# Hybrid mixer and product-key expert layer: first two input columns part by part, later columns between the recurrent gates, four query columns ahead of the second norm

## The chip, the cores and the metric

The kernel runs on one core of a Trainium2 chip. The metric is device time in microseconds (us), as the median of several runs. Engines are written as the profile writes them: PE is the matmul engine TensorE (PEld its weight loads), DVE is VectorE, ACT is ScalarE, POOL is GpSimd, SP is SyncE, which here only issues DMAs. Each engine takes its instructions in the order of its own queue. An instruction whose input isn't ready holds up everything behind it on its engine.

## The reference, cut to what matters

```python
# x: 512 tokens of 1024 values; rnn width 1280 in 10 blocks of 128
n = rms_norm(h, norm_mix)
a_x, a_b, a_c, r_x, r_y, g_a, g_b = split(n @ w_in)       # 60 columns of 128
y_a = (a_b * conv3(a_c * a_x)) @ w_out_a
r_c = conv4(r_x) + rnn_conv_b
r = sigmoid(blockdiag(r_c, w_rg) + b_rg); i = sigmoid(blockdiag(r_c, w_ig) + b_ig)
a = exp(-8 * r * softplus(-lam)); b = sqrt(1 - a*a) * i * r_c
r_h = scan(h_t = a_t * h_{t-1} + b_t)
y_b = (gelu(r_y) * r_h) @ w_out_b
h = h + (sigmoid(g_a) * y_a + sigmoid(g_b) * y_b) @ w_o
n = rms_norm(h, norm_ffn)
q = n @ w_q                                               # 16 columns, 2 per head
# per head: scores against two sets of 128 keys, top 16 of each, top 16 of the sums,
# softmax, then gelu(u . n) * v over the chosen experts of 16384
out = rms_norm(h + peer(n), norm_final)
```

## The kernel before, in words

Values are kept with channels on the 128 partitions and the 512 tokens along the row, so a vector of 1024 channels is eight parts. A matmul of two float32 matrices is made of three matmuls of a narrower float type: each operand is split into a high part (a copy by ACT, `whi` for weights) and the rest (a subtraction, `wlo`, by DVE, or by POOL for `w_q`), by `split` in lines 70 to 75. `mm3` in lines 83 to 89 runs the three products for each of the eight parts. What the text calls a column is one output block of 128 channels: 24 matmuls into one of the eight PSUM banks, which `bank` hands out in rotation over a string of bank numbers. Its weights come by `weights`: a DMA of 512 KB into one of four `raw` buffers, then the split into one of three pairs of `whi` and `wlo`. So the split of a column's weights waits until the column three places earlier is done on PE.

The mixer (lines 143 to 328) starts with the six early columns 24 to 29 of `w_in` (the first six blocks of `r_x`). They are taken of x times the norm's weights (tiles `xg`, `q_hi`, `q_lo`, made part by part) ahead of the division by the root mean square. `rms` squares the eight parts on ACT, sums them on DVE and POOL, adds over the partitions by two matmuls with `ones` and ends in `rstd`. `norm` then makes the normed values `n_hi` and `n_lo`, which every later column (`proj`) reads. For each of the ten recurrent blocks j (lines 199 to 228) the column is scaled by `rstd` into `pad` (on DVE for the six early ones, a copy on ACT for the others). Then come the convolution `rc` (one step on POOL, three on DVE), its split `rch`, `rcl`, the split of the gate weights (two tiles `tmp`), the six gate matmuls of line 219, sigmoids `lr` and `lx`, a tanh `lt`, and a product `lx` on DVE. Then follow the gated convolution (columns 16, 0 and 8 plus i), the recurrence, and the output columns. At the end of the mixer stands the second norm, with `NQ` columns of queries taken ahead of it in the same manner as the early ones (lines 320 to 328). The keys are loaded into a pool that takes over the mixer's memory (lines 398 to 400).

The scheduler of the framework sets the order of each engine's queue from the order of the code and from the buffers. After the mixer come eight heads of top-16 selection (with expert columns `ut` of 384 tokens laid between), the building of the gate matrix, and 128 rounds of expert output; nothing of the code there changes but where the first queries come from.

Of the kernel before, what the change touches and what calls it, by code (L numbers as in the profile page):

```python
# [11 lines left out]
F32 = mybir.dt.float32  # L12
F32R = mybir.dt.float32r
# [28 lines left out]
GSC = 32768.0  # L42
RN = 2.0
NEARLY = 6
NQ = 2
AR = 20
AD = 4
UP = 24
# [6 lines left out]
def layer(ctx: ExitStack, tc: tile.TileContext, a):  # L55
# [39 lines left out]
    def col(name, i):  # L95
        c = C_VEC[name] + i
        return vec[:, c : c + 1]
# [13 lines left out]
    ascr = dram.tile([P, P, ND], F32, name="ascr")  # L111

    ALLB = "01234567"

    def rms(src, pool, late):
        sums = [pool.tile([P, S], F32, tag=("rch", "rcl")[i], name="ssum", bufs=1) for i in range(2)]
        for k in range(KD):
            sq, e = sums[k // 4], V if late or k < 4 else G
            if k % 4 == 0:
                A.activation(sq, src[:, k, :], AF.Square)  # L120
            else:
                s = pool.tile([P, S], F32, tag="tmp", name="sqk", bufs=3)
                A.activation(s, src[:, k, :], AF.Square)
                e.tensor_add(sq, sq, s)
        ps = bank(ALLB)
        for i in range(2):
            T.matmul(ps, ones, sums[i], start=i == 0, stop=i == 1)
        rstd = pool.tile([P, S], F32, tag="rstd", name="rstd", bufs=1)
# [13 lines left out]

    with tc.tile_pool(name="mix", bufs=1) as mp:
        h = mp.tile([P, KD, S], F32, name="h")
        w0 = weights(a["w_in"][24], KD)
        for k in range(KD):
            SP.dma_start(h[:, k, :], a["x"][:, k, :])
        p_hi = mp.tile([P, KD, S], F32R, tag="p_hi", name="n_hi")
        p_lo = mp.tile([P, KD, S], F32R, tag="p_lo", name="n_lo")

        for k in range(KD):
            n = mp.tile([P, S], F32, tag="tmp", name="xg", bufs=3)
            V.tensor_scalar_mul(n, h[:, k, :], col("nm", k))
            A.activation(q_hi[:, k, :], n, AF.Copy)  # L154
            V.tensor_sub(q_lo[:, k, :], n, q_hi[:, k, :].bitcast(F32))
        xg = ([q_hi[:, k, :] for k in range(KD)], [q_lo[:, k, :] for k in range(KD)])
        rstd = rms(h, mp, False)
        early = []
        for j in range(NEARLY):
            ps = bank(ALLB)  # L160
            mm3(ps, w0 if j == 0 else weights(a["w_in"][24 + j], KD), xg)
            early.append(ps)
        norm(h, rstd, "nm", p_hi, p_lo, mp)
        n1 = ([p_hi[:, k, :] for k in range(KD)], [p_lo[:, k, :] for k in range(KD)])

        def proj(i):
            ps = bank(ALLB)
            mm3(ps, weights(a["w_in"][i], KD), n1)
            return ps

# [73 lines left out]


        for i in range(KD):
            ps_c = proj(16 + i)
            ac = mp.tile([P, S], F32, tag="tmp", name="ac", bufs=3)
            A.activation(ac, ps_c, AF.Copy)
            ps_x = proj(i)  # L250
# [7 lines left out]
            ps_b = proj(8 + i)  # L258
# [58 lines left out]
            A.activation(hgs[0][i], n, AF.Copy)  # L317
            V.tensor_sub(hgs[1][i], n, hgs[0][i].bitcast(F32))

        rstd = rms(h, mp, True)  # L320
        qearly = []
        for i in range(NQ):
            ps = bank(ALLB)
            mm3(ps, weights(a["w_q"][i], KD, G), hgs)
            q = qp.tile([P, S], F32, tag="q", name="q", bufs=NQ)
            V.tensor_mul(q, ps, rstd)
            qearly.append(q)
        norm(h, rstd, "nf", q_hi, q_lo, mp)
# [69 lines left out]
    with tc.tile_pool(name="top", bufs=1) as rp:  # L398
# [77 lines left out]
        for hd in range(H):  # L476
            qs = []
            for s in range(2):
                if 2 * hd + s < NQ:
                    qs.append(qearly[2 * hd + s])  # L480
                    continue
                pq = bank("23")
                mm3(pq, weights(a["w_q"][2 * hd + s], KD, G), n2)
                q = rp.tile([P, S], F32, tag="q", name="q", bufs=4)
                A.activation(q, pq, AF.Copy)
                qs.append(q)
            for t in order:
                psc = bank("45")
# [219 lines left out]
```

## Time and profile before

| | |
|---|---|
| time, median of 3 runs (lowest to highest) | 1835.59 us (1829.76 to 1838.79) |
| the profiled execution: its time, its span | 1833.47 us, 1831.7 us |
| granted TensorE clock, mean of the span | 0.975 |
| busy share: PE, PEld, DVE, ACT, POOL | 95%, 83%, 70%, 41%, 18% |
| chain that ended last, by engine | PE 78%, DVE 9%, DMA 8%, ACT 3%, issue 2% |

The span runs from the first to the last instruction; 1.8 us of the profiled time lie outside it. A busy share is a mean over stages, so where an engine stands still has to be looked up by stage. The granted clock is 1.0 where TensorE has its full 2.4 GHz and 0.5 where it has 1.2 GHz.

### The profile page before, as it was taken

The page shows a single profiled execution, that of the slowest core. Times are in us where ns is not written, and L with a number is a line of the kernel's source. Part 1 is how long each engine was busy: PE and PEld are TensorE (multiplying, and loading weights), DVE is VectorE, ACT ScalarE, POOL GpSimd, SP SyncE. Part 2 cuts the span into 40 slices and gives each one's busy share as a digit, 9 for nine tenths or more (in the row PEclk, how much of TensorE's full clock was granted, in tenths as well). Part 3 has the DMA queues.
Part 4 walks back from the last instruction along what each step waited for, and adds up shares of the span by engine and source line. Part 5 has one row for each costly group of instructions (what it writes and reads, how often), then busy time and mean ns, then how long its engine had stood idle before and what let it go on. Part 6 is the DMA issues. An engine that isn't in the chain of part 4 may idle for free.

```text
span 1831.7 us, 24059 instructions
## 1 busy us (share of the span) xinstructions
PE 1748.9 (95%) x8861; PEld 1520.1 (83%) x8861; DVE 1283.4 (70%) x2340; ACT 757.9 (41%) x1282; POOL 338.3 (18%) x266
## 2 busy tenths in 40 slices
PE   7899999999989999899999799999899999899898
PEld 5588888888878888899999688888787888788786
DVE  8857543223567668999999677787676876787673
ACT  5545333222334335555555343343343433444353
POOL 1200000000035553022322112122121221122100
PEclk9899999999999999999999899999999999999899
DMA  4222322333333334679899998898898988898872
GB/s 165 80 84 92 104 86 87 103 109 98 121 104 112 104 110 150 202 275 360 345 370 368 358 324 304 310 345 308 286 319 296 328 301 289 298 346 313 288 231 77
DMA packets 147846, 410.06 MB, mean 224 GB/s; under 512 B 11536, under 2 KB 78864, under 8 KB 129680
## 3 DMA queue, kind: packets, MB, share of 16 engines
q1 hardware_dynamic: 129296, 274.30, 45.1%
q0 software_dynamic: 18432, 134.23, 19.0%
q8 instruction: 69, 1.13, 0.2%
q14 instruction: 49, 0.40, 0.1%
HBM read 366.93 MB, written 41.55 MB: 223 GB/s over the span
## 4 chain that ended last, share of the span: by engine, by line
PE 78%; DVE 9%; DMA 8%; ACT 3%; issue 2%; POOL 0%; DVEq 0%; SPq 0%; ACTq 0%; POOLq 0%
PE ps L88 53%; PE acc L618 21%; DMA back<-ascr 4%; DVE wlo L74 3%; DMA gt<-gscr 2%; PE ps L556 1%; PE ps L557 1%; ACT whi L73 1%; PE ps L490 1%; DMA gscr<-stg 1%; DVE rc L210 1%; ACT w_hi L73 1%; DVE gel L611 1%; DVE junk L386 1%; PE ps L219 1%
## 5 line engine op out<-in xcount | busy, mean ns | idle before, releaser
L73 ACT ACTIVATE whi<-raw 128x1024 fp32r<-128x1024 f32 (+1 forms) x364 | 380.9, 1046 | 714.0 <-PE ps L88 471.6
L74 DVE TENSOR_TENSOR wlo<-raw,whi 128x1024 fp32r<-128x1024 f32 (+1 forms) x328 | 392.6, 1200 | 230.7 <-ACT whi L73 229.9
L88 PE MATMUL ps<-q_hi,whi 128*128 128x384 f32 (+1 forms) x1248 | 442.9, 355 | 13.5 <-ACT q_hi L154 7.6
L88 PE MATMUL ps<-q_hi,wlo 128*128 128x384 f32 (+1 forms) x1248 | 436.9, 351 | 4.9 <-DVE wlo L74 4.9
L88 PE MATMUL ps<-q_lo,whi 128*128 128x384 f32 (+1 forms) x1248 | 436.9, 351 | 2.8 <-DVE q_lo L138 2.5
L379 POOL DMA_INDIRECT row<-uv,uidx x128 | 209.6, 1637 | 770.1 <-DVE yg L373 760.7
L618 PE MATMUL acc<-whi,w_hi 128*128 128x512 f32 x768 | 246.3, 402 | 36.2 <-ACT w_hi L73 36.2
L88 PEld LDWEIGHTS ps<-q_hi,whi 128*128 128x128 f32 x1248 | 238.1, 191 | 27.4 <-ACT q_hi L154 8.1
L88 PEld LDWEIGHTS ps<-q_hi,wlo 128*128 128x128 f32 x1248 | 238.3, 191 | 16.0 <-DVE wlo L74 5.8
L88 PEld LDWEIGHTS ps<-q_lo,whi 128*128 128x128 f32 x1248 | 238.4, 191 | 14.8 <-DVE q_lo L138 2.9
L618 PE MATMUL acc<-wlo,w_hi 128*128 128x512 f32 x768 | 243.0, 398 | 2.2 <-DVE wlo L74 2.2
L618 PE MATMUL acc<-whi,w_lo 128*128 128x512 f32 x768 | 241.7, 396 | 0.0
L618 PEld LDWEIGHTS acc<-whi,w_hi 128*128 128x128 f32 x768 | 145.7, 193 | 68.0 <-ACT w_hi L73 42.5
L618 PEld LDWEIGHTS acc<-wlo,w_hi 128*128 128x128 f32 x768 | 148.1, 193 | 34.8 <-DVE wlo L74 2.7
L618 PEld LDWEIGHTS acc<-whi,w_lo 128*128 128x128 f32 x768 | 147.5, 192 | 31.9
L88 PE MATMUL ps<-n_hi,whi 128*128 128x512 f32 x432 | 169.0, 391 | 0.0
L88 PE MATMUL ps<-n_hi,wlo 128*128 128x512 f32 x432 | 168.7, 390 | 0.0
L88 PE MATMUL ps<-n_lo,whi 128*128 128x512 f32 x432 | 168.6, 390 | 0.0
L373 DVE SCALAR_TENSOR_TENSOR yg<-row,dots,yg 128x1024 f32<-128x1024 f32 x128 | 163.6, 1278 | 0.0
L386 DVE SCALAR_TENSOR_TENSOR junk<-row,n2tok 128x1024 bf16<-128x1024 f32 x128 | 155.8, 1217 | 0.0
L74 POOL TENSOR_TENSOR wlo<-raw,whi 128x1024 fp32r<-128x1024 f32 x36 | 87.1, 2419 | 347.8 <-ACT whi L73 341.4
L88 PEld LDWEIGHTS ps<-n_hi,whi 128*128 128x128 f32 x432 | 81.5, 189 | 17.6 <-ACT lr L221 0.6
(208 smaller groups left out, 1878.2 us busy)
## 6 DMA issues: line engine op xcount, KB each, us to landing
raw<-ut SPq DMA_DIRECT2D x128, 512.0 KB, 5.5
raw<-uv SPq DMA_DIRECT2D x128, 512.0 KB, 5.8
raw<-w_in SPq DMA_DIRECT2D x60, 512.0 KB, 3.3
gscr<-stg SPq DMA_DIRECT2D x12, 2048.0 KB, 10.4
gt<-gscr SPq DMA_DIRECT2D x32, 768.0 KB, 8.1
ascr<-gel SPq DMA_DIRECT2D x62, 192.0 KB, 5.5
back<-ascr SPq DMA_DIRECT2D x62, 192.0 KB, 6.4
raw<-w_q SPq DMA_DIRECT2D x16, 512.0 KB, 3.7
```

The lines of the kernel that those rows point to most:

```text
L73: A.activation(hi, raw, AF.Copy)
L74: (lo_eng or V).tensor_sub(lo, raw, hi.bitcast(F32))
L88: T.matmul(ps, w[x][:, i, :], r[y][i], start=first and n == 0, stop=last and n == 3 * k - 1)
L210: V.scalar_tensor_tensor(rc, pad[:, w : w + S], col("rw", 4 * j + w), rc, op0=ALU.mult, op1=ALU.add)
L219: T.matmul(pg, x[:, s * P : (s + 1) * P], y, start=n == 0, stop=n == 2)
L373: V.scalar_tensor_tensor(yg, r[:, D:], dots[:, i : i + 1], yg, op0=ALU.mult, op1=ALU.add)
L379: ins = G.indirect_dma_start(out=r, out_offset=None, in_=a["uv"], in_offset=bass.IndirectOffsetOnAxis(ap=uidx[:, i : i + 1], axis=0))
L386: V.scalar_tensor_tensor(junk, r[:, :D], 1.0, n2tok, op0=ALU.mult, op1=ALU.mult, accum_out=dots[:, i : i + 1])
L490: T.matmul(psc[:, s * P : (s + 1) * P], qs[s][:, t * P : (t + 1) * P], keys[:, 2 * hd + s, :], start=True, stop=True)
L556: T.matmul(o, e2[:, ti // 2, :, ti % 2], eh[:, ti // 2, :, ti % 2], start=True, stop=False)
L557: T.matmul(o, e2[:, ti // 2, :, ti % 2], el[:, ti // 2, :, ti % 2], start=False, stop=True)
L618: T.matmul(acc[t][f], w[x][:, t * P : (t + 1) * P], vf[y][:, f * S : (f + 1) * S], start=nout == 0 and (x, y) == (0, 0), stop=nout == P - ...
```

## The change

- The first part of x is fetched ahead of the first weights, and the second column's weights after three parts. The first two columns run part by part together: as soon as a part of `xg` is split, PE takes its three products for column 24 and for column 25. Columns 26 to 29 follow whole.
- `rms` is cut into `squares` (all sums on DVE) and `inverse_rms`. The first norm's square sums come behind the third column's weights, and its two `ones` matmuls behind the third column. The six early columns keep banks 0 to 5.
- In each recurrent step j one later column is put ahead of the gates: 30 to 33, then 16, 0, 8, 17, 1, 9, in banks 0 to 5. The gates use banks 6 and 7. A column of step j needs the bank that the column six places earlier has left.
- The first step of the convolution goes from POOL to ACT.
- Four query columns (was two) run ahead of the second norm, the `ones` matmuls behind the first of them. The products with `rstd` of the third and fourth are made later, at head 1.

```diff
-NQ = 2
+NQ = 4
+NS = 2
...
-    def rms(src, pool, late):
+    def squares(src, pool):
...
-            sq, e = sums[k // 4], V if late or k < 4 else G
+            sq = sums[k // 4]
...
-                e.tensor_add(sq, sq, s)
-        ps = bank(ALLB)
+                V.tensor_add(sq, sq, s)
+        return sums
+
+    def inverse_rms(sums, names):
+        ps = bank(names)
...
+        SP.dma_start(h[:, 0, :], a["x"][:, 0, :])
         w0 = weights(a["w_in"][24], KD)
-        for k in range(KD):
+        for k in range(1, KD):
             SP.dma_start(h[:, k, :], a["x"][:, k, :])
...
+            if k == 2:
+                w1 = weights(a["w_in"][25], KD)
+        early = [bank(COLS) for _ in range(NEARLY)]
         for k in range(KD):
...
+            for ps, w in zip(early, (w0, w1)):
+                mm3(ps, [x[:, k : k + 1, :] for x in w], ([q_hi[:, k, :]], [q_lo[:, k, :]]), k == 0, k == KD - 1)
...
-        rstd = rms(h, mp, False)
-        early = []
-        for j in range(NEARLY):
-            ps = bank(ALLB)
-            mm3(ps, w0 if j == 0 else weights(a["w_in"][24 + j], KD), xg)
-            early.append(ps)
...
+        for j in range(2, NEARLY):
+            w = weights(a["w_in"][24 + j], KD)
+            if j == 2:
+                sums = squares(h, mp)
+            mm3(early[j], w, xg)
+            if j == 2:
+                rstd = inverse_rms(sums, "67")
...
+        columns = iter([o_rx + j for j in range(NEARLY, KR)] + [c + i for i in range(2) for c in (16, 0, 8)])
+        held = {}
         for j in range(KR):
-            ps = early[j] if j < NEARLY else proj(o_rx + j)
+            ps = early[j] if j < NEARLY else held.pop(o_rx + j)
...
-            G.tensor_scalar(rc, pad[:, 3 : S + 3], col("rw", 4 * j + 3), col("rb", j), op0=ALU.mult, op1=ALU.add)
+            A.activation(rc, pad[:, 3 : S + 3], AF.Identity, scale=col("rw", 4 * j + 3), bias=col("rb", j))
...
+            c = next(columns)
+            held[c] = proj(c, COLS)
             gates = []
...
-                pg = bank(ALLB)
+                pg = bank("67")
...
-            ps_c = proj(16 + i)
+            ps_c = held.pop(16 + i) if i < 2 else proj(16 + i)
...
-        rstd = rms(h, mp, True)
+        sums = squares(h, mp)
+        qps = []
+        for i in range(NQ):
+            ps = bank("0123"[i])
+            mm3(ps, weights(a["w_q"][i], KD, G), hgs)
+            qps.append(ps)
+            if i == 0:
+                rstd = inverse_rms(sums, "67")
         qearly = []
-        for i in range(NQ):
-            ps = bank(ALLB)
-            mm3(ps, weights(a["w_q"][i], KD, G), hgs)
...
+        for ps in qps[:NS]:
...
+                if n < NQ:
+                    V.tensor_mul(q, qps[n], rstd)
+                else:
```

What moves in the queues is shown at three places. The first is the start of PE's queue. Before, column 24 (`ps_163`) runs alone; its first two parts:

```order
L88 MATMUL ps_163<-q_hi_75,whi_89 128x512
L88 MATMUL ps_163<-q_lo_76,whi_89 128x512
L88 MATMUL ps_163<-q_hi_75,wlo_90 128x512
L88 MATMUL ps_163<-q_hi_75,whi_89 128x512
L88 MATMUL ps_163<-q_lo_76,whi_89 128x512
L88 MATMUL ps_163<-q_hi_75,wlo_90 128x512
```

Of the change, from the second part of column 24 (`ps_107`) on, with column 25 (`ps_108`):

```order
L89 MATMUL ps_107<-q_hi_75,whi_90 128x512
L89 MATMUL ps_107<-q_lo_76,whi_90 128x512
L89 MATMUL ps_107<-q_hi_75,wlo_91 128x512
L89 MATMUL ps_108<-q_hi_75,whi_98 128x512
L89 MATMUL ps_108<-q_lo_76,whi_98 128x512
L89 MATMUL ps_107<-q_hi_75,whi_90 128x512
L89 MATMUL ps_108<-q_hi_75,wlo_99 128x512
L89 MATMUL ps_108<-q_hi_75,whi_98 128x512
L89 MATMUL ps_108<-q_lo_76,whi_98 128x512
L89 MATMUL ps_108<-q_hi_75,wlo_99 128x512
L89 MATMUL ps_107<-q_lo_76,whi_90 128x512
L89 MATMUL ps_107<-q_hi_75,wlo_91 128x512
```

Two columns now share the parts as they come; before, the second began when the first had seven parts behind it.

The second place is PE's queue behind the last early column. Before, the gate matmuls (L219) of block 0 (`ps_430`, `ps_436`) and of block 1 (`ps_463`) stand one behind the other:

```order
L88 MATMUL ps_312<-q_hi_75,wlo_316 128x512
L219 MATMUL ps_430<-rch_420,tmp_426 128x512
L219 MATMUL ps_436<-rch_420,tmp_426 128x512
L219 MATMUL ps_430<-rcl_421,tmp_426 128x512
L219 MATMUL ps_430<-rch_420,tmp_427 128x512
L219 MATMUL ps_436<-rcl_421,tmp_426 128x512
L219 MATMUL ps_436<-rch_420,tmp_427 128x512
L219 MATMUL ps_463<-rch_453,tmp_459 128x512
L219 MATMUL ps_463<-rcl_454,tmp_459 128x512
L219 MATMUL ps_463<-rch_453,tmp_460 128x512
L219 MATMUL ps_469<-rch_453,tmp_459 128x512
```

Of the change, from the last matmul of column 30 (`ps_430`) over the gates of block 0 (L236) to column 31 (`ps_494`):

```order
L89 MATMUL ps_430<-n_hi_193,wlo_434 128x512
L236 MATMUL ps_461<-rch_420,tmp_426 128x512
L236 MATMUL ps_461<-rcl_421,tmp_426 128x512
L236 MATMUL ps_461<-rch_420,tmp_427 128x512
L236 MATMUL ps_467<-rch_420,tmp_426 128x512
L236 MATMUL ps_467<-rcl_421,tmp_426 128x512
L236 MATMUL ps_467<-rch_420,tmp_427 128x512
L89 MATMUL ps_494<-n_hi_193,whi_497 128x512
L89 MATMUL ps_494<-n_lo_194,whi_497 128x512
L89 MATMUL ps_494<-n_hi_193,wlo_498 128x512
```

Each group of six gate matmuls now has a column of 24 on either side. DVE's queue of the change for one such step (convolution of block 7, a column's weight split, product and maximum of block 5, splits of block 7):

```order
L224 SCALAR_TENSOR_TENSOR rc_863<-pad_860,vec_66,rc_863 128x512 x3
L75 TENSOR_TENSOR wlo_1010<-raw_1007,whi_1009 128x1024
L242 TENSOR_TENSOR lx_855<-lx_855,rc_799 128x512
L252 TENSOR_SCALAR lt_857<-lt_857 128x512
L75 TENSOR_TENSOR rcl_869<-rc_863,rch_868 128x512
L75 TENSOR_TENSOR tmp_875<-graw_872,tmp_874 128x256
L224 SCALAR_TENSOR_TENSOR rc_927<-pad_924,vec_66,rc_927 128x512 x3
```

The third place is PE's queue at the second norm. Before, the second query column (`ps_3689`, of `lr` and `lx`) is followed by columns that read the normed `q_hi`, `q_lo`:

```order
L88 MATMUL ps_3689<-lr_3624,wlo_3693 128x512
L88 MATMUL ps_3896<-q_hi_75,whi_3892 128x384
L88 MATMUL ps_3929<-q_hi_75,whi_3925 128x384
L88 MATMUL ps_3956<-q_hi_75,whi_3959 128x512
L88 MATMUL ps_3896<-q_lo_76,whi_3892 128x384
```

Of the change, the ends of the four query columns (`ps_3650`, `ps_3687`, `ps_3718`, `ps_3749`) with the `ones` matmuls (L132):

```order
L89 MATMUL ps_3650<-lr_3624,wlo_3654 128x512
L132 MATMUL ps_3681<-ssum_3628,ones_68 128x512
L132 MATMUL ps_3681<-ssum_3629,ones_68 128x512
L89 MATMUL ps_3687<-lr_3351,whi_3690 128x512
...
L89 MATMUL ps_3687<-lr_3624,wlo_3691 128x512
L89 MATMUL ps_3718<-lr_3351,whi_3721 128x512
...
L89 MATMUL ps_3718<-lr_3624,wlo_3722 128x512
L89 MATMUL ps_3749<-lr_3351,whi_3752 128x512
...
L89 MATMUL ps_3749<-lr_3624,wlo_3753 128x512
L89 MATMUL ps_3958<-q_hi_75,whi_3954 128x384
```

72 matmuls that don't need the norm now stand between the `ones` matmuls and the first that does; before it was 24 and a few. From row 2297 of PE's queue on (the expert columns between heads 0 and 1) its order is the same before and after, and so it is on the other engines after the first heads.

## Rows read from the trace of the kernel before

**Rows 1.** Page, part 1: busy us of TensorE (share of the span), instructions.

```profile
PE 1748.9 (95%) x8861; PEld 1520.1 (83%) x8861; DVE 1283.4 (70%) x2340; ACT 757.9 (41%) x1282; POOL 338.3 (18%) x266
```

**Rows 2.** Stretches: busy us of PE, PEld, DVE, ACT, POOL; PEclk; DMA share; GB/s.

```profile
7.58:20.91 13.33, 13.04 (x41) 9.31 (x41) 13.33 (x23) 10.05 (x18) 1.95 (x1) 1.00 0.85 311
20.91:28.28 7.37, 4.88 (x11) 2.60 (x11) 6.79 (x20) 2.48 (x3) 3.41 (x2) 0.77 0.23 81
50.72:66.42 15.70, 8.34 (x19) 4.37 (x17) 14.74 (x22) 8.61 (x13) 2.38 (x5) 0.65 0.36 117
66.42:107.19 40.77, 39.68 (x162) 30.19 (x162) 32.38 (x52) 25.01 (x43) 8.10 (x13) 0.97 0.22 71
107.19:135.30 28.11, 28.11 (x125) 23.27 (x124) 12.91 (x16) 9.98 (x14) 0.20 (x2) 1.00 0.30 94
```

**Rows 3.** Waits of PE, 50.7 to 107.2 us: total, times, longest.

```profile
PE ps L219 <- ACT rch L73: 3.6, 3, 2.9
```

**Rows 4.** Timeline of PE, 27 to 51 us: start, duration, instruction.

```profile
27.08 0.63 PE L88 MATMUL ps<-q_lo,whi 128*128 128x512 f32 x1
27.50 0.63 PE L88 MATMUL ps<-q_hi,wlo 128*128 128x512 f32 x1
...
28.51 0.40 PE L88 MATMUL ps<-q_hi,wlo 128*128 128x512 f32 x1
28.74 0.39 PE L88 MATMUL ps<-q_hi,whi 128*128 128x512 f32 x1
...
50.72 0.63 PE L219 MATMUL ps<-rch,tmp 128*128 128x512 f32 x2
```

**Rows 5.** Groups by line on DVE, 26 to 108 us: busy, mean ns, idle before.

```profile
L210 DVE SCALAR_TENSOR_TENSOR rc<-pad,vec,rc 128x512 f32<-128x512 f32 x30 | 22.4, 745 | 3.9 <-POOL rc L208 1.9 <-POOL pad L202 1.9
L74 DVE TENSOR_TENSOR wlo<-raw,whi 128x1024 fp32r<-128x1024 f32 x9 | 10.9, 1212 | 2.1 <-ACT whi L73 2.1
L74 DVE TENSOR_TENSOR rcl<-rc,rch 128x512 fp32r<-128x512 f32 x10 | 7.2, 724 | 0.4 <-ACT rch L73 0.4
L225 DVE TENSOR_TENSOR lx<-lx,rc 128x512 f32<-128x512 f32 x9 | 6.2, 686 | 4.1 <-ACT lx L221 4.1
L136 DVE SCALAR_TENSOR_TENSOR nk<-h,vec,rstd 128x512 f32<-128x512 f32 x8 | 5.5, 744 | 0.0
L138 DVE TENSOR_TENSOR n_lo<-nk,n_hi 128x512 fp32r<-128x512 f32 x8 | 5.2, 680 | 0.0
L74 DVE TENSOR_TENSOR tmp<-graw,tmp 128x256 fp32r<-128x256 f32 x10 | 4.5, 455 | 0.4 <-ACT tmp L73 0.4
L204 DVE TENSOR_TENSOR pad<-ps,rstd 128x512 f32<-128x512 f32 x6 | 4.1, 683 | 0.0
L234 DVE TENSOR_SCALAR lt<-lt 128x512 f32<-128x512 f32 x9 | 3.8, 418 | 0.0
L130 DVE RECIPROCAL rstd<-rstd 128x512 f32<-128x512 f32 x1 | 3.3, 3349 | 0.0
```

**Rows 6.** The same view on ACT, 30 to 108 us.

```profile
L221 ACT ACTIVATE lr<-ps,vec 128x512 f32<-128x512 f32 x10 | 6.9, 689 | 15.8 <-PE ps L219 15.8
L206 ACT ACTIVATE pad<-ps 128x512 f32<-128x512 f32 x4 | 2.3, 583 | 0.0
```

**Rows 7.** Timeline of PE around the second norm.

```profile
525.69 1.13 PE L127 MATMUL ps<-ssum,ones 128*128 128x512 f32 x2
...
563.93 1.16 PE L490 MATMUL ps<-keys,q 128*128 128x128 f32 x8
564.84 0.42 PE L88 MATMUL ps<-q_hi,wlo 128*128 128x384 f32 x1
```

**Rows 8.** Timeline of DVE: end of the second norm.

```profile
544.52 1.36 DVE L138 TENSOR_TENSOR q_lo<-nk,q_hi 128x512 fp32r<-128x512 f32 x2
```

**Rows 9.** Tile keys: its DMA (ns, first and last start us) and its landing.

```profile
L400 SPq DMA_DIRECT2D keys<-keys x1: 328/328/328, 546.0 to 546.0; - x1
DMA to landing us min/median/max: 4.8/4.8/4.8
```

More of the change, by code (lines that the diff above doesn't have):

```diff
@@ L113, in layer @@
     ALLB = "01234567"
-    def rms(src, pool, late):
+    COLS = "012345"
+    def squares(src, pool):
         sums = [pool.tile([P, S], F32, tag=("rch", "rcl")[i], name="ssum", bufs=1) for i in range(2)]
         for k in range(KD):
-            sq, e = sums[k // 4], V if late or k < 4 else G
+            sq = sums[k // 4]
             if k % 4 == 0:
@@ L123, in rms @@
                 A.activation(s, src[:, k, :], AF.Square)
-                e.tensor_add(sq, sq, s)
-        ps = bank(ALLB)
+                V.tensor_add(sq, sq, s)
+        return sums
+    def inverse_rms(sums, names):
+        ps = bank(names)
         for i in range(2):
             T.matmul(ps, ones, sums[i], start=i == 0, stop=i == 1)
-        rstd = pool.tile([P, S], F32, tag="rstd", name="rstd", bufs=1)
+        rstd = qp.tile([P, S], F32, tag="rstd", name="rstd", bufs=1)
         A.activation(rstd, ps, AF.Sqrt, bias=epst, scale=1.0 / D)
@@ L144, in layer @@
         h = mp.tile([P, KD, S], F32, name="h")
+        SP.dma_start(h[:, 0, :], a["x"][:, 0, :])
         w0 = weights(a["w_in"][24], KD)
-        for k in range(KD):
+        for k in range(1, KD):
             SP.dma_start(h[:, k, :], a["x"][:, k, :])
-        p_hi = mp.tile([P, KD, S], F32R, tag="p_hi", name="n_hi")
-        p_lo = mp.tile([P, KD, S], F32R, tag="p_lo", name="n_lo")
+            if k == 2:
+                w1 = weights(a["w_in"][25], KD)
+        early = [bank(COLS) for _ in range(NEARLY)]
         for k in range(KD):
@@ L155, in layer, with proj @@
             V.tensor_sub(q_lo[:, k, :], n, q_hi[:, k, :].bitcast(F32))
+            for ps, w in zip(early, (w0, w1)):
+                mm3(ps, [x[:, k : k + 1, :] for x in w], ([q_hi[:, k, :]], [q_lo[:, k, :]]), k == 0, k == KD - 1)
         xg = ([q_hi[:, k, :] for k in range(KD)], [q_lo[:, k, :] for k in range(KD)])
-        rstd = rms(h, mp, False)
-        early = []
-        for j in range(NEARLY):
-            ps = bank(ALLB)
-            mm3(ps, w0 if j == 0 else weights(a["w_in"][24 + j], KD), xg)
-            early.append(ps)
+        p_hi = mp.tile([P, KD, S], F32R, tag="p_hi", name="n_hi")
+        p_lo = mp.tile([P, KD, S], F32R, tag="p_lo", name="n_lo")
+        for j in range(2, NEARLY):
[5 more added lines that the diff above has]
+                rstd = inverse_rms(sums, "67")
         norm(h, rstd, "nm", p_hi, p_lo, mp)
         n1 = ([p_hi[:, k, :] for k in range(KD)], [p_lo[:, k, :] for k in range(KD)])
-        def proj(i):
-            ps = bank(ALLB)
+        def proj(i, names=ALLB):
+            ps = bank(names)
             mm3(ps, weights(a["w_in"][i], KD), n1)
@@ L246, in layer @@
         for i in range(KD):
-            ps_c = proj(16 + i)
+            ps_c = held.pop(16 + i) if i < 2 else proj(16 + i)
             ac = mp.tile([P, S], F32, tag="tmp", name="ac", bufs=3)
             A.activation(ac, ps_c, AF.Copy)
-            ps_x = proj(i)
+            ps_x = held.pop(i) if i < 2 else proj(i)
             pad = mp.tile([P, S + 4], F32, tag="pad", name="pad", bufs=2)
@@ L257, in layer @@
                 V.scalar_tensor_tensor(cv, pad[:, w : w + S], col("ca", 3 * i + w), cv, op0=ALU.mult, op1=ALU.add)
-            ps_b = proj(8 + i)
+            ps_b = held.pop(8 + i) if i < 2 else proj(8 + i)
             V.tensor_mul(cv, cv, ps_b)
@@ L318, in layer @@
             V.tensor_sub(hgs[1][i], n, hgs[0][i].bitcast(F32))
-        rstd = rms(h, mp, True)
+        sums = squares(h, mp)
[6 more added lines that the diff above has]
+                rstd = inverse_rms(sums, "67")
         qearly = []
-        for i in range(NQ):
-            ps = bank(ALLB)
-            mm3(ps, weights(a["w_q"][i], KD, G), hgs)
-            q = qp.tile([P, S], F32, tag="q", name="q", bufs=NQ)
+        for ps in qps[:NS]:
+            q = qp.tile([P, S], F32, tag="q", name="q", bufs=NS)
             V.tensor_mul(q, ps, rstd)
@@ L478, in layer @@
             for s in range(2):
-                if 2 * hd + s < NQ:
-                    qs.append(qearly[2 * hd + s])
+                n = 2 * hd + s
+                if n < NS:
+                    qs.append(qearly[n])
                     continue
-                pq = bank("23")
-                mm3(pq, weights(a["w_q"][2 * hd + s], KD, G), n2)
                 q = rp.tile([P, S], F32, tag="q", name="q", bufs=4)
-                A.activation(q, pq, AF.Copy)
+                if n < NQ:
+                    V.tensor_mul(q, qps[n], rstd)
+                else:
+                    pq = bank("23")
+                    mm3(pq, weights(a["w_q"][n], KD, G), n2)
+                    A.activation(q, pq, AF.Copy)
                 qs.append(q)
```

## The prediction

> **What bounds the kernel now.** I read the page first: TensorE is busy 95% of the span [rows 1], so time can be won only where PE stands, or where it runs at the lower of its two clocks. The view of stretches finds those places. From 107.19 us on the mixer is packed: 28.11 us busy of 28.11 [rows 2]. Ahead of that it is not. From 20.91 to 28.28 PE is busy 4.88 of 7.37 us at a granted clock of 0.77, from 50.72 to 66.42 it is busy 8.34 of 15.70 us at 0.65, while DVE is busy 14.74 of the 15.70 [rows 2]. The view of waits says what ends them in the second stretch, ACT's split `rch` for instance, three times and 2.9 us at the longest [rows 3]: the gates of the first recurrent blocks have no columns between them. The timeline gives PE's price at both clocks. Two matmuls of 512 tokens start 0.42 us apart at 27 us and 0.23 us apart at 28.5 us [rows 4]; the first is the 1.2 GHz level, the second the 2.4 GHz level. Around the second norm the reader sees the same in small: a `ones` product at 525.69, and the first matmul behind the scores of head 0 and the first half of head 1 only at 564.84 [rows 7].
>
> PE's queue holds the same matmuls before and after, so I compare the times at which PE reaches the same count. There are two such marks, and behind each of them PE has the same queue in both kernels.
>
> **The first mark: all 60 gate matmuls and ten later columns done.** Before, the last gate is done at 107.19, where the stretch begins [rows 2]. By the queue PE then has 118 of the 240 matmuls of the ten later columns behind it. The other 122 at 0.23 us are 28.1 us, so the mark is reached at 135.3.
>
> After, step by step:
> - The first two columns. Before, PE ran 41 matmuls in the 13.33 us from its first one on [rows 2]. I take the same pace for the 48 of the two columns: 13.33 x 48/41 = 15.6, so 23.2 us. The two columns are fed by the same splits as before and one weight split more on DVE (1.21 us, [rows 5]); the fetches differ by one place in the queue. Taken at nothing: the earlier fetch of x's first part, since the weights' split still has to end first.
> - The third column, 24 x 0.23 = 5.5, to 28.7. Behind it stand the two `ones` matmuls, 1.0 us each (the one at 525.69 lasts 1.13, [rows 7]), to 30.7. The three square sums that leave POOL for DVE cost 0.68 each like `n_lo` [rows 5]; they hide behind the third column. In the stretch from 20.91, where PE stood, POOL was still adding such sums (busy 3.41 us, [rows 2]); that stand is gone.
> - Three more columns, 72 x 0.23 = 16.6, to 47.3. Beside them runs the norm: square root 0.69 (as the sigmoid `lr` with its column operand, [rows 6]), reciprocal 3.35, eight parts at 0.744 + 0.680, and the split 1.21 of the first later column [rows 5]: 30.7 + 0.7 + 3.35 + 11.4 + 1.2 = 47.3. Both chains end together, so each us that either is longer is a us lost. The norm is what comes late next. Before, PE reached this place at 50.72 [rows 4].
> - Ten steps of a column and a pair of gates, 30 x 0.23 = 6.9 us of PE each, to 116.3. For this DVE has to keep up. A step costs it three convolution steps, a weight split, `rcl`, `lx`, `tmp`, `pad` (six times only) and `lt`: 2.24 + 1.21 + 0.72 + 0.69 + 0.46 + 0.68 + 0.42 = 6.4 us [rows 5]. That is under 6.9, though not by much. ACT was busy 25.01 of 40.77 us while the gates of eight blocks ran [rows 2]. Its new step has no row; below it lies a copy of 0.58, above it a sigmoid with a column operand, 0.69 [rows 6]. I take the upper one, since it has column operands too: ten of them are 7 us, and ahead of `lr` alone ACT was idle for 15.8 us [rows 6].
> - The tenth column's successor needs a bank that the gated convolution must first read out. It stands behind DVE's last steps; I put 1 us there. The mark comes at 117.3.
>
> The gain is 135.3 - 117.3 = 18.0 us. At best PE never waits and is at full clock throughout, 7.6 + 444 x 0.23 + 2 = 111.7, a gain of 23.6. At worst the clock and the gate chain (rivals below) take 7 and 15 us of it back.
>
> Here the Trainium skill weighs against one part. Its page "ScalarE: Activation LUTs", section "Rules for kernel authors", puts multiplies and adds on VectorE and not on ScalarE. The rows say otherwise in this place: one more convolution step of 0.745 us would lift DVE's step from 6.4 to 7.2 us, above PE's 6.9, and cost some 3 us over ten steps. I go by the rows.
>
> **The second mark: PE's row 2297, between heads 0 and 1.** Before it is reached at 564.84 [rows 7]. After, everything up to the second `ones` product at 525.69 is unchanged, since the sums end when they ended. Then 526.7 + 72 x 0.23 = 543.3 for the three further query columns. DVE's work on the norm is not longer than before and ends at 545.9 [rows 8]. The first expert column reads the parts one after the other, 24 x 0.17 = 4.1 us (384 of 512 tokens, three quarters of 0.23), so it meets the last part when that is there: the norm is hidden. With ten more matmuls PE is at 549.1. Next in its queue are scores, which need the keys. These are fetched into the mixer's memory once the norm has left it, at 546.0 before, and land 4.8 us later [rows 9]: 550.8. So the keys are late next, and PE stands 1.7 us. From there 16 score rows at 0.91 us for four (the gap between the last two of [rows 7]) and 22 expert matmuls at 0.17 make 7.4: the mark comes at 558.2.
>
> The gain is 564.8 - 558.2 = 6.6 us. Without the wait for keys it is 8.3. In SP's queue the fetch of the keys now stands behind one more weight fetch, which waits for POOL; if that holds it up by 3 us, 3.6 are left. The two products with `rstd` that move to DVE behind the norm are taken as 0.68 each, like `pad` [rows 5]; they end at 547.3, ahead of the keys, and cost nothing unless the keys come early.
>
> **The sum.** 18.0 + 6.6 = 24.6 us. From the second mark on each stage starts from the one ahead of it, and no queue differs after the first heads, so I carry it to the end undiminished. The profiled execution took 1833.5 us, which gives 1809 us; the median of the runs shown is 1835.6, 2 us above it.
>
> **The rivals.**
> - *The clock stays low at the start.* The trace: after PE had stood in 20.91 to 28.28 the matmuls came 0.42 us apart at first [rows 2, 4]. After, the first parts come in more slowly for two columns, since PE waits for two weight splits. If all 48 run 0.42 us apart, they take 20.2 us, 4.6 more than in my sum, and if the third column starts so, up to 4.6 more. I take 7: 1816 us. Against it: 41 matmuls in 13.33 us were already fed part by part. Chance 0.12. The Trainium skill, page "TensorE: Matmul & The Clock Gate", section "Part 1: The HAM clock gate", says that the throttled state is the default and that activity releases it, which is the ground for this case. The slow pace behind the stand [rows 4] agrees with it.
> - *The gates wait for their own chain.* `rch` and `rcl` have one buffer, so the split for block j+1 starts only when the gates of j are done, behind two sigmoids and a tanh on ACT. Four ACT instructions of 0.69 [rows 6] and `rcl` of 0.72 [rows 5] are 3.5 of the 5.5 us that a column covers. If a weight split and the two instructions of a later block stand ahead in ACT's queue, some 2 us are left over; with 1.5 us lost in each of ten steps it is 1824 us. Before, PE waited for this very split [rows 3]. Chance 0.12.
> - *More than I count.* Both marks at their best, 23.6 + 8.3: 1801 us. It needs the norm to end ahead of PE and the keys not to be waited for. Chance 0.08.
> - *Given back later.* If a later stage is set by a transfer that does not start earlier, the gain ends there: 1833 us. For it speaks only that I price no later stage; against it, that all later fetches are issued in an order that hangs on PE's and DVE's progress. Chance 0.07.
> - *Slower.* One mechanism: in the ten steps PE's queue is in order, and a column now stands ahead of each pair of gates, waiting for a bank that DVE's `pad` must free. If DVE needs more than 6.9 us a step, PE stands in every step, and if its clock then falls as it did from 50.72 to 66.42, a step costs 30 x 0.42 = 12.6 us, 5.7 more. That turns the sum to a loss from five such steps on; with all ten it is 1866 us. DVE was busy 32.38 of 40.77 us while the later blocks ran [rows 2], so I give it 0.04.
>
> **How the numbers follow.** The likeliest case has 0.57 and its own range 1803 to 1815. A measurement of this kernel can tell about 0.5% from no change, 9.2 us: faster means under 1826.4, slower over 1844.8. Faster: 0.57, 0.12, 0.08 and two thirds of the gate chain's 0.12, together 0.85. Same: the rest of that and the case given back, 0.11. Slower 0.04. The range 1798 to 1825 takes in the first four cases but for their outer ends, and leaves out 0.07 + 0.04 and some 0.08 of these ends.
>
> **What would show it.** Right: two columns done near 23 us; no stand of PE for POOL; column 30 begun at 47 to 48; ten regular steps of 6.9 us with a clock of 1.0; gates done near 116; the keys' landing as the last wait around the second norm; row 2297 some 25 us earlier in all. Wrong: steps of 8 us or more with waits for `rch` or `pad`; matmuls 0.42 us apart beyond 20 us; a longer stand at the gate matrix or in the expert stage that eats the 25 us.

## The result and the profile after

The change takes 1810.92 us in the median of 4 runs (1809.08 to 1812.24) against 1832.67 us (4 runs, three of them those of the section on the time before), a ratio of 0.9877, 95% interval 0.9845 to 0.991: 1.2% faster. The profiled execution took 1809.08 us, with a span of 1807.4 us. TensorE does the same 8861 matmuls as in [rows 1], in 12 us less of busy time:

```profile
PE 1736.7 (96%) x8861; PEld 1515.1 (84%) x8861; DVE 1286.5 (71%) x2345; ACT 763.8 (42%) x1290; POOL 320.2 (18%) x253
```

Stretches of the kernel after, columns as in [rows 2]. The first three are the first two columns (all but their last matmul, which starts at 23.45), the way to column 30, and the ten steps of a column and a pair of gates. The last two lie in front of and behind the first scores:

```profile
7.43:23.45 16.02, 14.77 (x48) 10.80 (x49) 14.48 (x28) 9.84 (x17) 0.00 (x0) 1.00 0.72 275
23.45:47.38 23.93, 23.93 (x103) 18.97 (x101) 22.13 (x43) 12.95 (x19) 0.00 (x0) 1.00 0.23 72
47.38:115.67 68.29, 68.29 (x302) 56.23 (x300) 59.63 (x90) 47.62 (x75) 1.24 (x11) 1.00 0.34 110
530.85:534.03 3.18, 0.17 (x1) 0.03 (x1) 0.00 (x0) 1.20 (x2) 3.18 (x2) 1.00 0.68 271
534.03:538.90 4.87, 4.87 (x25) 4.87 (x26) 3.73 (x26) 1.54 (x4) 1.83 (x3) 0.65 0.73 238
```

From 23.45 to 115.67 PE doesn't stand once, at a granted clock of 1.00; before, it was busy 8.34 of 15.70 us at 0.65 in the middle of it [rows 2]. The fourth line is what is left: PE busy 0.17 of 3.18 us, and behind that a clock of 0.65. The timeline of PE shows the same place row by row (start, duration, instruction, idle time before), with the second `ones` product ahead of it and, at 543.26, PE's row 2297, the second mark:

```profile
506.62 1.12 PE L132 MATMUL ps<-ssum,ones 128*128 128x512 f32 x2 [1.07 <-DVE ssum L126]
...
530.68 0.34 PE L89 MATMUL ps<-q_hi,whi 128*128 128x384 f32 x1
534.03 1.13 PE L517 MATMUL ps<-keys,q 128*128 128x128 f32 x8 [3.01 <-issue]
534.91 0.51 PE L89 MATMUL ps<-q_lo,whi 128*128 128x384 f32 x1
535.22 0.52 PE L89 MATMUL ps<-q_hi,wlo 128*128 128x384 f32 x1
...
543.26 0.34 PE L89 MATMUL ps<-q_hi,wlo 128*128 128x384 f32 x1
...
1005.67 1.22 PE L645 MATMUL acc<-whi,w_hi 128*128 128x512 f32 x2 [8.23 <-ACT w_hi L74]
```

PE stands 3.01 us ahead of the scores. The matmuls of 384 tokens that follow come 0.31 us apart instead of 0.17. The last row is the first product of the expert output; before, it comes at 1027.51.

The row of the stand names no releaser (`issue`). That PE waits for the keys shows in the second profile of the change (`after_again`), which has their landing: fetched at 528.3 us, landed 4.7 us later, at 533.0, and PE's first score at 533.19:

```profile
L423 SPq DMA_DIRECT2D keys<-keys x1: 328/328/328, 528.3 to 528.3; - x1
DMA to landing us min/median/max: 4.7/4.7/4.7
533.19 1.02 PE L517 MATMUL ps<-keys,q 128*128 128x128 f32 x7 [2.57 <-issue]
```

The 21.8 us that the medians differ by build up over three marks with the same work behind them, to within one row: 19.1 at the second `ones` product (525.69 before, [rows 7]; row 2151 of PE's queue before, 2152 in the change), 21.6 at row 2297 (564.84), 21.8 at the first product of the expert output. In the profiled pair the end is 24.3 us earlier. The last 2.5 us are scatter: from that product to the end the 14 profiles of this study take between 796.9 and 812.0 us, in no order that follows the kernels, whereas the expert output repeats to 0.6 us in the change and to 0.3 in another kernel that ran twice. I therefore read the experiments at two marks, the second `ones` product (all of the mixer) and the first product of the expert output, and the times beside them. Each ratio is to the runs of the kernel before in the same set (medians 1832.67, 1832.13, 1830.11 and 1834.15 us), so it isn't the quotient of two medians of the table.

| kernel | second `ones` | expert output | between | median, us (runs) | ratio to before, 95% interval |
|---|---|---|---|---|---|
| before | 525.69 | 1027.51 | 501.8 | 1832.67 (4) | |
| the change | 506.62 | 1005.67 | 499.1 | 1810.92 (4) | 0.9877, 0.9845 to 0.991 |
| `mixer_only` | 506.24 | 1007.86 | 501.6 | 1814.62 (6) | 0.991, 0.988 to 0.9941 |
| `norm2_only` | 524.12 | 1020.64 | 496.5 | 1825.36 (12) | 0.9971, 0.9946 to 0.9995 |
| `start_whole` | 509.93 | 1011.29 | 501.4 | 1815.11 (9) | 0.9911, 0.9885 to 0.9938 |
| `gates_plain` | 522.28 | 1018.86 | 496.6 | 1827.39 (10) | 0.9981, 0.9954 to 1.0008 |
| `step_dve` | 508.53 | 1010.48 | 502.0 | 1815.27 (6) | 0.9916, 0.9888 to 0.9945 |
| `step_pool` | 507.74 | 1005.43 | 497.7 | 1812.85 (2) | 0.989, 0.9852 to 0.9929 |
| `early_keys` | 505.86 | 1005.57 | 499.7 | 1811.75 (6) | 0.9903, 0.9871 to 0.9934 |
| `scores_later` | 507.54 | 1000.87 | 493.3 | 1804.33 (4) | 0.986, 0.9811 to 0.9909 |
| `split_dve` | 505.45 | 1003.79 | 498.3 | 1806.78 (4) | 0.9868, 0.9808 to 0.9928 |
| `pool_idle` | 505.91 | 998.47 | 492.6 | 1803.76 (2) | 0.9841, 0.9806 to 0.9875 |
| `scores_again` | 506.53 | 1000.57 | 494.0 | 1810.65 (5) | 0.9877, 0.9852 to 0.9902 |
| `after_again` | 506.21 | 1005.06 | 498.9 | 1808.68 (6) | 0.9879, 0.9851 to 0.9907 |

How finely the marks can be read shows where the code is the same. The start scatters: in the eight profiles that share the change's mixer, column 30 (row 147) begins between 46.60 and 48.27 us. From there to row 447 all eight take 68.28 to 68.32 us, and the kernel before 84.13. From row 447 to the second `ones` product it is 390.8 to 391.0 us (389.7 in the two kernels with splits of query weights on DVE). From row 2297 to the expert output, where the queues are the same (in `early_keys` from row 2302), it is 460.9 to 463.2. So two kernels can differ by some 2 us at a mark of the table by scatter alone; inside the mixer, between two rows, a tenth of a us can be read.

### The profile page after: what moved, and what is told of

Its sections match the earlier page's. It is cut to its first block, busy times and chain, and to the rows that moved or that the text cites. A ratio compares the mean times of both kernels' runs of the same rounds, so it can differ in the third digit from the quotient of the medians.

```text
span 1807.4 us, 24072 instructions
## 1 busy us (share of the span) xinstructions
PE 1736.7 (96%) x8861; PEld 1515.1 (84%) x8861; DVE 1286.5 (71%) x2345; ACT 763.8 (42%) x1290; POOL 320.2 (18%) x253
## 3 DMA queue, kind: packets, MB, share of 16 engines
q0 software_dynamic: 18432, 134.23, 19.2%
## 4 chain that ended last, share of the span: by engine, by line
PE 78%; DMA 9%; DVE 8%; issue 2%; ACT 2%; SPq 0%; DVEq 0%; ACTq 0%
PE ps L89 55%; PE acc L645 19%; DMA back<-ascr 5%; DMA gt<-gscr 3%; DVE wlo L75 3%; PE ps L583 1%; PE ps L584 1%; PE ps L517 1%; ACT whi L74 1%; PE ps L236 1%; DVE gel L638 1%; DMA gscr<-stg 1%; ACT w_hi L74 1%; DVE junk L409 1%; DVE nk L141 0%
## 5 line engine op out<-in xcount | busy, mean ns | idle before, releaser
L89 PE MATMUL ps<-q_hi,whi 128*128 128x384 f32 (+1 forms) x1232 | 436.4, 354 | 11.6 <-ACT whi L74 8.9
L89 PE MATMUL ps<-q_hi,wlo 128*128 128x384 f32 (+1 forms) x1232 | 430.0, 349 | 6.1 <-DVE wlo L75 6.1
L89 PE MATMUL ps<-q_lo,whi 128*128 128x384 f32 (+1 forms) x1232 | 429.8, 349 | 0.3 <-DVE q_lo L143 0.3
L89 PEld LDWEIGHTS ps<-q_hi,whi 128*128 128x128 f32 x1232 | 234.6, 190 | 24.3 <-ACT whi L74 10.2
L89 PEld LDWEIGHTS ps<-q_hi,wlo 128*128 128x128 f32 x1232 | 234.2, 190 | 17.1 <-DVE wlo L75 8.1
L89 PEld LDWEIGHTS ps<-n_hi,wlo 128*128 128x128 f32 x432 | 81.1, 188 | 17.5 <-DVE wlo L75 0.4
```

The costliest lines, as they stand in the source:

```text
L89: T.matmul(ps, w[x][:, i, :], r[y][i], start=first and n == 0, stop=last and n == 3 * k - 1)
```

## The experiments

**One part alone.** `mixer_only` is the change without its second norm (`NQ = 2`, products with `rstd` as before); `norm2_only` is the kernel before with the change's second norm, of which these are the main lines:

```diff
-NQ = 2
+NQ = 4
+NS = 2
...
+        for i in range(NQ):
+            ps = bank("0123"[i])
+            mm3(ps, weights(a["w_q"][i], KD, G), hgs)
+            qps.append(ps)
+            if i == 0:
+                rstd = inverse_rms(sums, "67")
```

> The changed mixer, but the second norm and its two query columns as before. Theory read from the two traces: the mixer's part is worth 19.6 us (end of the gates and ten later columns at 115.67 us instead of 135.3) and nothing of it is lost up to the end. So 1832.7 - 19.6 = 1813 us, PE's row 2297 near 545.2, and PE stands at the second norm as it did before (the gap between the second ones product and row 2297 stays 39.2 us). Rival, the split of the prediction: the second norm is worth 6.6 us, so of the whole gain of 21.7 only 15.1 is the mixer's: 1817.6 us.

> The kernel before with only the four query columns ahead of the second norm. Theory from the traces: it is worth 2.0 us, 1830.7 us; PE stands about 3 us ahead of the first scores for the keys, then runs a few us at the lower clock, and row 2297 comes near 562.8. Rival, the prediction's term: the keys cost 1.7 us only and row 2297 comes at 558.2, 1826 us. A third outcome, no gain or a loss (1833 or more), would say that the two parts only go together.

The mixer alone brings the `ones` product 19.5 us forward, and 19.7 are left at the expert output. That is the theory; the rival's 15.1 is out. `norm2_only` met neither. Its time is the rival's, but not the way to it: it reaches the `ones` product 1.6 us earlier, though nothing of the mixer differs (its first gate starts at 49.08 us instead of 50.72, scatter of the start), and from there to the expert output it needs 5.3 us less than before, not 2.0 or 6.6. At row 2297 it is 3.7 us (35.42 from the `ones` product against 39.15). Its PE timeline shows why it isn't the same experiment:

```profile
547.98 0.44 PE L89 MATMUL ps<-q_lo,whi 128*128 128x384 f32 x1 [2.01 <-DVE q_lo L142]
...
554.78 1.13 PE L503 MATMUL ps<-keys,q 128*128 128x128 f32 x8
```

PE stands for the norm's last part, but not for the keys: the scheduler has put the first scores behind two whole expert columns here, and in the change behind one and 10 of 24 rows of the next. At row 2297 the second part is worth 3.7 us in this order and 2.5 in the change's, at the expert output 5.3 and 2.8. Such a difference is near the scatter; the next kernel tests it.

**The order of the scores.** `scores_later` gives the change that order:

```diff
+            if hd == 0:
+                lag_tiles(AR // H)
             for t in order:
...
+                    if hd == 0 and t == 3 and s == 0:
+                        tc.keep_in_program_order(i)
```

> The change, with the first scores of head 0 put 14 rows later in PE's queue, behind two whole expert columns. Theory: the keys land when they did (near 533.8 us), but PE now has 14 more expert matmuls of 0.17 us, 2.4 us, to do before it needs them. Of the stand of 3.0 us some 0.6 is left, the clock does not fall behind it (another 1.7 us), and the first product of the expert output comes near 1001.7 instead of 1005.7: 1807 us. Rival: what follows hangs on the chain from the keys' landing over scores and top-16, and PE's free time is only moved behind the scores; then that mark stays at 1005.7 and the time at 1811 us.

The PE timeline of `scores_later` from its first score on, and its stretch of 5 us there:

```profile
534.67 1.13 PE L519 MATMUL ps<-keys,q 128*128 128x128 f32 x8 [0.30 <-PE ps L89]
535.55 0.42 PE L89 MATMUL ps<-q_hi,whi 128*128 128x384 f32 x1
535.81 0.34 PE L89 MATMUL ps<-q_lo,whi 128*128 128x384 f32 x1
535.99 0.34 PE L89 MATMUL ps<-q_hi,wlo 128*128 128x384 f32 x1
```
```profile
535.00:540.00 5.00, 5.00 (x41) 4.79 (x40) 3.51 (x24) 3.18 (x9) 4.09 (x4) 1.00 0.84 247
```

The stand is 0.30 us instead of 3.01, the matmuls behind it are 0.17 us apart, the clock of the stretch is 1.00. From the `ones` product to the expert output it takes 493.3 us, 5.8 less than the change. Of these, 4.2 are there at row 2297 (32.41 us from the `ones` product against 36.64), and 3.9 in a second pair of profiles (32.30 against 36.22); the rest lies where the queues are the same. The theory holds, and the rival's mark of 1005.7 is out: the stand and the clock behind it were the loss. Both kernels then ran once more on one chip:

> The kernel with later scores once more, beside the change on the same chip. Theory: 4 to 6 us faster than the change, 1805 us. Rival: the difference of the medians so far (1804.3 against 1810.9) is scatter of the expert rounds, and the two agree within 2 us.

> The change once more, unaltered, for the comparison on one chip: 1811 us, and the second ones product, the stand ahead of the keys (3 us) and the lower clock behind it as in its first profile. If the clock does not fall this time, the first product of the expert output comes some 2 us earlier against the ones product than the 499.0 us of the first profile.

The marks repeat: 1000.57 against 1005.06 us, and in the change PE again stood 2.6 us for the keys and ran at 0.71 from 535 to 540. The times don't show it: 1810.65 against 1808.68 us, in ranges of 9 and 13 us. Over both sets of runs the medians are 1805.7 (9 runs) and 1810.1 (10 runs). That 4.5 to 4.8 us are won by 1000 us is shown; that the kernel is faster by as much at the end is not, since the expert rounds scatter by more.

**The keys early.** `early_keys` keeps the keys of head 0 in memory of their own:

```diff
+    keys0 = qp.tile([P, 2, P], F32, name="keys0")
...
+        SP.dma_start(keys0, a["keys"][:, 0:2])
```

> The change, with the keys of head 0 (128 KB) in memory of their own, fetched during the mixer, and only the rest in the reused memory. Theory: the late landing of the keys is what ate the second part's gain, by 3.0 us of standing and some 2.5 us of lower clock behind it. Without it PE runs the scores of head 0 directly behind the query columns at full clock, row 2297 comes 4 to 5.5 us earlier than 543.3, and the time is 1805.5 to 1807 us. Rival: PE then stands for DVE instead (the end of the norm, or the keys of head 1, which land when they did) and the time stays at 1810 to 1812 us.

PE's rows of the first scores in `early_keys`:

```profile
523.32 1.05 PE L520 MATMUL ps<-keys,q 128*128 128x128 f32 x8
...
528.39 2.07 PE L520 MATMUL ps<-keys,q 128*128 128x128 f32 x8 [3.50 <-ACT sc L522]
```

The rival's outcome by another way. The scheduler moved the scores ahead of the expert columns, the third score then needed a bank that ACT's copy `sc` had to empty, and `sc` stood in ACT's queue behind the norm's `q_hi`. PE stood 3.50 us, the clock fell to 0.61 from 530 to 535, and the mark is the change's to 0.1 us.

**What made the norm late.** In the change the keys are fetched at 528.7 us, as soon as the norm's last `q_lo` is done. The view of the tile `nk` (DVE; min/median/max ns, first and last start) shows why that is late:

```profile
L141 DVE SCALAR_TENSOR_TENSOR nk<-h,vec,rstd x8: 739/740/2920, 513.9 to 526.5; 128x512 f32<-128x512 f32 x8
```

Six of the eight `nk` take 0.74 us; two take 2.90 and 2.92. In the timelines of DVE and of POOL the two groups of three that hold them last 4.22 and 4.25 us, and beside each POOL splits a weight:

```profile
513.90 4.22 DVE L141 SCALAR_TENSOR_TENSOR nk<-h,vec,rstd 128x512 f32<-128x512 f32 x3
...
519.85 4.25 DVE L141 SCALAR_TENSOR_TENSOR nk<-h,vec,rstd 128x512 f32<-128x512 f32 x3
```
```profile
514.25 2.66 POOL L75 TENSOR_TENSOR wlo<-raw,whi 128x1024 fp32r<-128x1024 f32 x1 [5.45 <-ACT whi L74]
519.82 2.41 POOL L75 TENSOR_TENSOR wlo<-raw,whi 128x1024 fp32r<-128x1024 f32 x1 [2.91 <-ACT whi L74]
```

A group without a split beside it lasts 2.07 (`mixer_only`, at 519.83). The norm before, which ends in [rows 8], had one long group, beside a split of 2.81 us that began at 533.54:

```profile
533.39 4.17 DVE L136 SCALAR_TENSOR_TENSOR nk<-h,vec,rstd 128x512 f32<-128x512 f32 x3
```

The change has two. With two query columns more ahead in POOL's queue, its fifth and its sixth split fall beside the norm, before only the fifth.

`split_dve` puts the splits of the third and fourth query column on DVE (`V if i > 1 else G`). `pool_idle` does so with all four and with four expert columns, on top of the later scores:

```diff
-            mm3(ps, weights(a["w_q"][i], KD, G), hgs)
+            mm3(ps, weights(a["w_q"][i], KD, V), hgs)
...
-        u = weights(a["ut"][j], KD, G if j in LAG[:AR] else V)
+        u = weights(a["ut"][j], KD, G if j in LAG[4:AR] else V)
```

> The change, with the weight splits of the third and fourth query column on DVE instead of POOL; the scheduler then also puts the first scores as late as in the kernel with later scores, so the two are to be compared with each other. Theory: POOL's splits of 2.4 to 2.7 us run beside the norm and slow DVE's nk from 0.69 to 1.40 us in six of eight parts (4.2 us saved), against 2.4 us for the two splits on DVE: the norm ends 1.8 us earlier, near 525.5, and the keys land near 531.5. Rival: nk is slow for another reason; then DVE's two more splits make the norm end 2.4 us later and the mark of the expert output comes later than in the other kernel.

> The kernel with later scores, and all weight splits that POOL made around the second norm (four query columns, the first four expert columns) on DVE, so that POOL stands still from the mixer to the norm's end. Theory: POOL's splits beside it are what doubles DVE's nk in the second norm; then all eight nk take 0.69 us, three of them 2.06 instead of 4.2. The splits on DVE cost 1.22 us each, so the norm need not end earlier. Rival: nk is slow by itself at that place (its operands, ACT's copies beside it); then three of them still take 4.2 us.

`split_dve` took away the wrong splits. Those that lie beside `nk` are the two expert columns', and POOL made them at 512.37 and 517.93, again beside two groups of 4.2 us; PE then stood 2.0 us for the norm. So the rival's outcome came (expert output at 1003.79 us, in `scores_later` at 1000.87) with `nk` as slow as ever, and that left its cause open. (The 1.40 us in six parts of the expectation is the mean of such groups; it is two parts at 2.9.) `pool_idle` settles it. With POOL still until 525.19, every `nk` takes its 0.75 us (the same view):

```profile
L141 DVE SCALAR_TENSOR_TENSOR nk<-h,vec,rstd x8: 743/748/751, 512.5 to 521.2; 128x512 f32<-128x512 f32 x8
```

PE has no wait at all from 500 to 550 us, the norm ends 19.1 us behind the `ones` product instead of 22.0, and the expert output comes 7.2 us earlier than in the change, 2.1 to 2.4 of them beyond `scores_later`, whose order it shares. The two timed runs (1803.76) are too few to rank it.

**Start, gates and the moved step.** `start_whole` puts back the old start, `gates_plain` takes the columns out from between the gates (with the banks as before), `step_dve` and `step_pool` move the first convolution step:

```diff
-            A.activation(rc, pad[:, 3 : S + 3], AF.Identity, scale=col("rw", 4 * j + 3), bias=col("rb", j))
+            V.tensor_scalar(rc, pad[:, 3 : S + 3], col("rw", 4 * j + 3), col("rb", j), op0=ALU.mult, op1=ALU.add)
```

> The change, with its start undone: early columns whole, one after the other, and three square sums on POOL as before; columns still between the gates. Theory: the start alone is worth 2.9 us (PE had 144 matmuls behind it at 46.69 instead of 49.57), so the gates end near 118.3 instead of 115.4 and the time is 1814 us. Rival: the norm on DVE ends late in both, so PE would only stand in front of column 30 after the faster start, and undoing it costs under 1 us.

> The change, with the columns taken out from between the gates and the banks as before; start, ACT's convolution step and second norm as in the change. Theory: the columns between the gates are worth the rest of the first mark, 16.7 us: the mark of the expert output near 1022.4 us, the time near 1827.6 us. Rival: part of the old wait was POOL's convolution step (1.9 us each time); with the step on ACT the gates come sooner and only 10 to 13 us are lost, 1821 to 1824 us.

> The change, with the first step of the convolution on DVE instead of ACT. Theory of the prediction: DVE's step of the recurrent blocks grows by 0.75 us from 6.4 to 7.2, above the 6.8 us that PE's step takes, so the gates end some 3 us later than 115.67 and the time is near 1814 us. Rival, by the row after: the step on ACT takes 0.81 us, more than the 0.75 on DVE, and DVE stood for ACT's weight splits; with ACT relieved nothing is lost or up to 1 us is gained, 1810 to 1811 us.

> The change, with the first convolution step back on POOL. It took 1.36 us there in the kernel before. Theory of the cover: a block's convolution has a whole column of 5.5 us between its neighbours now, so a step that is 0.55 us longer is hidden; the second ones product stays within 1 us of 506.6. Rival: DVE's convolution waits for POOL in every block, DVE's step passes PE's 6.8 us, and the ones product comes 3 to 8 us later.

At the `ones` product the start is worth 3.3 us (509.93 against 506.62) and the columns between the gates 15.7 (522.28). Together they are 19.0 of the 19.1. The start's share rests on one pair of profiles and has the start's scatter: `start_whole` begins column 30 at 50.95 us, 2.7 to 4.4 later than the eight above. At the expert output it is 5.6 us behind the change, since its keys took 6.45 us to land (4.7 to 6.6 in the profiles that show it), PE stood 4.31 us for them and the clock was 0.75 behind the stand. In `gates_plain` PE stands where it did before, although POOL has no step there any more (its waits from 48 to 107 us, and a stretch to set beside the third of [rows 2]):

```profile
PE ps L234 <- ACT tmp L74: 4.7, 2, 2.5
PE ps L234 <- ACT rch L74: 3.8, 1, 3.8
```
```profile
50.58:66.42 15.84, 10.42 (x20) 5.97 (x21) 14.95 (x23) 10.05 (x16) 0.30 (x3) 0.50 0.36 116
```

So its rival is out at this mark. Its expert output is only 13.2 us later than the change's; it has the late order of the scores (496.6 us between the marks, like `norm2_only`).

In `step_dve` PE waits 1.44 us inside column 30 for DVE's `wlo` of it and then not at all, 68.00 of 68.00 us busy. The step on DVE has a form of its own and takes 0.54 us, not 0.75; on ACT it takes 0.81. The rows are a stretch and a group of `step_dve`, and ACT's group of the change (ten of 0.812 us):

```profile
50.00:118.00 68.00, 68.00 (x300) 56.13 (x300) 61.47 (x97) 40.61 (x66) 1.38 (x11) 1.00 0.32 109
```
```profile
L222 DVE TENSOR_SCALAR rc<-pad,vec 128x512 f32<-128x512 f32 x9 | 4.9, 544 | 0.0
```
```profile
L222 ACT ACTIVATE rc<-pad,vec 128x512 f32<-128x512 f32 x10 | 8.1, 812 | 2.4 <-DVE pad L218 2.4
```

From column 30 to row 447 it costs 1.4 us (69.74 against 68.29), by one wait and not by ten longer steps; the `ones` product is 1.9 us later, the rest by the start. So the theory fails, though its 1814 us were nearly met: the 2.9 us that follow come from the second norm, where PE ran at 0.73 from 506 to 512 us and stood 3.4 us for the keys. The rival, nothing lost, is out too. `step_pool` costs 1.6 us over the same rows (69.89), nearly all at a single wait of 1.1 for `rcl` in the first block: from there on the column covers it.

## Why the prediction was right, and where not

The time forecast was 1809 us, and it came at 1810.9. The gain was forecast at 24.6 us and came at 21.8: the two terms under it were off by 1.2 and 4.1 us, in opposite directions, so part of the agreement is luck. That the profiled execution took 1809.08 is luck altogether, as 2.5 us of its lead are the scatter behind the last mark.

- *The first mark* was forecast to gain 18.0 us and gained 19.2: row 447 begins at 115.67 us, and before at 134.85. (The 135.3 of the prediction, and with it the 19.6 of an expectation, count the last 122 matmuls at 0.23 us; they took 0.227.) At the `ones` product 19.1 of it are left. Two columns were done at 23.7 (forecast 23.2) and column 30 began at 47.38 (47.3). A step took 6.8 us, not 6.9, and for a bank, put at 1 us, PE didn't wait. The split into start and gates, 3.4 and 14.6 us by those times, measured 3.3 and 15.7.
- *The moved step.* ACT's 0.69 was too low (0.81), which cost nothing, ACT being busy 47.62 of 68.29 us. The 3 us that the step would cost on DVE were too many (1.4); what failed there is its price of 0.745, taken from another form. The Trainium skill's rule on its page "ScalarE: Activation LUTs", section "Rules for kernel authors", is borne out as to the engine's own time, 0.54 us on DVE against 0.81. Neither place matters for PE by more than some 2 us.
- *The second mark* is where the prediction went wrong: 6.6 us forecast, 2.5 measured (21.6 - 19.1). The step that failed first is "DVE's work on the norm is not longer than before". A second split on POOL falls beside `nk`, which costs 2.2 us (0.4 come back, as `nk` begins that much sooner behind the `ones` product), and the norm ends later: the keys are fetched at 528.7 instead of 526.9 (546.0 of [rows 9] less 19.1), 1.8 us. From there to PE's first score it took 5.3 us, 0.5 more than the landing of [rows 9], and that is scatter (4.7 in the second profile). The lower clock behind the stand cost 1.8 (9.2 us from the scores to row 2297, forecast 7.4); the prediction had no term for it. These three are the 4.1 us missing. That a split lengthens `nk` was to be read before the change too: the group at 533.39 lasts 4.17 us. The Trainium skill's page "SBUF — State Buffer", section "SBUF: two separate sides", says that a DVE operation with two SBUF inputs and a GpSimd operation that reads SBUF lock each other out for a whole instruction rather than share. The two `nk` of 2.90 and 2.92 us beside splits of 2.66 and 2.41 agree, and so do the eight of 0.75 with POOL still. The prediction did not weigh it.
- That the keys would be late next was right, and `scores_later` shows that it was the order of PE's queue, not the keys alone, that made PE stand for them. The prediction read that order and didn't ask what lay ready behind the waiting scores.
- *The rivals.* The clock did stay low at the start, matmuls 0.43 us apart until 16 us, but not beyond the pace that was counted. The gates never waited for their own chain. Nothing was given back later: between the second `ones` product and the expert output the change is 2.8 us faster than before. DVE's step never passed PE's (busy 59.63 of 68.29 us).

## What to carry to other kernels

Put independent matmuls between a chain's links and price the gain at equal counts in the PE queue; in the mixer that was good to 10%, where the scatter of the total hides 5 us. Where work goes ahead of a norm to hide it, check what its own preparation does to the norm: here a split on POOL cost the norm on DVE 2.2 us, more than the 1.22 of the same split on DVE. And look at what stands behind a waiting instruction in an in-order queue: moving four products 14 rows back gave more than fetching their operand earlier.

## What was not expected of the hardware

- Up to 16 us the matmuls of 512 tokens come 0.43 us apart, the pace of the lower level [rows 4]; from there on 0.23. The column of the granted clock reads 1.00 over both, but the first record of the clock in this trace stands at 16.28 us: ahead of it the column rests on no record, and the pace tells the level.
- Behind the two `ones` products, with waits of 0.60 and 1.07 us in both, the pair at 508.53 in `step_dve` took 1.94 us (granted clock 0.73), that of the change 1.12. So a fall of the clock behind waits of that length is not certain either way; what decides it was not tried.
